# The inverse of each RWKV chunk multiplied into beta and the output weights ahead of the chain

## The chip, the core and the metric

The kernel runs on one core of a Trainium2 chip. The metric is the device time of one execution in microseconds (us). Engines are named as the profile names them: PE is the matrix engine (PEld its weight loads), DVE the vector engine, ACT the scalar engine, POOL and SP the other two; here SP issues nearly all DMAs.

## The reference, cut to what matters

The program is one layer of a bidirectional hybrid model: a modulated norm, an input projection, an RWKV-7 branch (16 heads of 64), a gated DeltaNet branch (8 heads of 128), a gated merge, and an MLP, over 256 latent and 256 context tokens. The change is inside the RWKV branch, whose recurrence for each head and direction is

```python
def step(s, inp):
    dec_t, k_t, v_t, kk_t, b_t = inp[:5]
    sa = jnp.einsum('bhvk,bhk->bhv', s, kk_t)
    s = (s * dec_t[:, :, None, :] - sa[..., None] * b_t[:, :, None, :]
         + v_t[..., None] * k_t[:, :, None, :])
    if with_out:
        return s, jnp.einsum('bhvk,bhk->bhv', s, inp[5])
    return s, None
```

It runs forwards and backwards over the context (state only) and then over the latent tokens (state and output). Each step reads the state that the step before left.

## The kernel before

The recurrence is done in chunks of 64 tokens: 8 chunks a direction, 4 of context and 4 of latent tokens. Two heads are worked on together as a *pair*, one in partitions 0 to 63 and one in 64 to 127; there are 8 pairs, and each has both directions. Within a chunk the dependence of the tokens on each other is a triangular system, so the work of a pair is in three generators:

- `prep2` makes, for all chunks, the decayed keys and betas (`ea`, `eb`), the triangular matrices (`dg` and `off`, their diagonal and off-diagonal 32x32 blocks), the transposed beta and key rows `bt`, and the output weights `mb`. Its products go to accumulators `pg`, of which there are two (`psg`, bufs=2).
- `inv2` inverts the 16 triangular 64x64 matrices of the pair: `tri_inv` does the 32x32 blocks in 31 steps on DVE, then two sets of small products (L818, L828) make the off-diagonal block, ACT copies the parts together into `ti`, and transposes of the values go into `vt`. Its accumulator `pr` is one (`psr`, bufs=1).
- `chain` goes through the 8 chunks in order, both directions side by side. A chunk has three products, each of which needs the one before: old state and values with `ea` or `eb` (L878), copied to `rs`; the inverse `ti` with `rs` (L896), copied into the tile `vu`; `bt` with `vu` (L912), from which DVE makes the next state. For latent chunks L917 and L919 add the output, the latter from `mb` and `vu`.

The function `weave` sets the order in which all of this is written. Its dense stream is the weight products of the projections: `mm3` (L239 to L241) does each weight tile in three products of a high and a low part, which `wgran` makes from the loaded weights, the high part on ACT (L226), the low part on DVE (L227). Into this stream `weave` puts steps of three lanes: the chains (first RWKV, then DeltaNet), the inverses, the preparations. A `yield` names how much dense work should pass until a lane's next step: CW = 1.5 between the products of a chain, times F_C = 1.5 for the chain's lane; Y[2] and Y[3] in `inv2`, times F_I = 0.7. Lanes wait for each other through sets: `chain` of a pair begins when the pair is in `done` (its `inv2` has ended), `inv2` of pair p when p - 2 is in `read` (that chain has ended), `prep2` likewise. The framework then orders the instructions of each engine by this order and by what is ready. When the RWKV chains are over, the DeltaNet heads follow with lanes of the same kind (`gprep`, `ginv`, `gchain`); the dense stream goes on with gates and up-projections `upa` (L1271 ends one). A DeltaNet head that ends before the gates do is written to memory and read again as `yr`, a later one goes straight to its place. Behind the weave come the branch merge, the output projection and the MLP, which the change doesn't touch.

## Time and profile before

| what | before |
| --- | --- |
| median of 3 runs | 2323.81 us (2322.46 to 2330.43) |
| the profiled execution's own time | 2331.12 us |
| its span | 2329.3 us |
| PE busy | 2218.4 us, 95% |
| DVE busy | 1581.7 us, 68% |
| ACT busy | 1353.9 us, 58% |
| DMA | 179 GB/s on average |

The span is the time from the first to the last recorded instruction of the profiled execution; the device time has a little around it. "Busy" is the union of an engine's instructions. A matrix product of two float32 operands is two PE instructions in the trace, one with the split weight products or a transpose is one.

### The profile page before, as it was taken

What the parts mean: (1) busy time and instruction counts of PE and PEld (TensorE: products, weight loads), DVE (VectorE), ACT (ScalarE), POOL (GpSimd) and SP (SyncE); (2) the same over time, 40 slices, a digit from 0 to 9 for tenths busy, and PEclk for the clock granted to TensorE, in tenths of its full rate; (3) what the DMA queues carried; (4) which work ended last, traced back from release to release, by engine and by line L of the source; (5) the groups of instructions that cost most, each with busy time, mean ns of one, the idle gap of its engine ahead of it and who ended that gap; (6) DMA issues with size and microseconds to landing.
All of it is one profiled execution on the core that took longest, in us unless ns stands there. A gap on an engine that the chain in (4) does not pass through costs nothing.

```text
span 2329.3 us, 45293 instructions
## 1 busy us (share of the span) xinstructions
PE 2218.4 (95%) x16886; PEld 1799.4 (77%) x16886; DVE 1581.7 (68%) x3590; ACT 1353.9 (58%) x3003; POOL 158.6 (7%) x343
## 2 busy tenths in 40 slices
PE   5989999999999999999999989999999999999997
PEld 1566676767677776778887889879998888999886
DVE  2366875858686867678577777776886555666555
ACT  3244758575758575766665676456555444555544
POOL 0000021111111121111000000000000000000000
PEclk9998999999999999999999999999999999999999
DMA  9953333423333333457676554875776666555654
GB/s 368 329 177 128 104 111 106 141 90 122 109 128 117 121 118 116 132 186 246 200 234 204 173 170 152 291 242 183 262 259 199 193 193 193 183 182 181 192 195 146
DMA packets 184372, 417.95 MB, mean 179 GB/s; under 512 B 15380, under 2 KB 37076, under 8 KB 183128
## 3 DMA queue, kind: packets, MB, share of 16 engines
q1 hardware_dynamic: 183576, 414.02, 54.3%
q8 instruction: 132, 2.16, 0.4%
q10 hardware_dynamic: 576, 1.05, 0.1%
q14 instruction: 88, 0.72, 0.1%
HBM read 399.63 MB, written 15.38 MB: 178 GB/s over the span
## 4 chain that ended last, share of the span: by engine, by line
PE 72%; ACT 8%; DVE 6%; DMA 4%; issue 2%; SPq 0%; DVEq 0%; ACTq 0%; POOL 0%; POOLq 0%
PE dacc L239 14%; PE dacc L240 13%; PE dacc L241 12%; PE dacc L1430 3%; PE pm L1428 3%; PE pm L1429 3%; PE pm L1430 3%; PE dacc L1428 3%; PE dacc L1429 3%; DMA raw<-in_mod_w_dram 2%; PE vacc L296 2%; DVE lo L227 2%; ACT hi L226 1%; PE cb L878 1%; PE pg L748 1%
## 5 line engine op out<-in xcount | busy, mean ns | idle before, releaser
L226 ACT CAST hi<-raw 128x512 fp32r<-128x512 f32 (+1 forms) x1032 | 628.1, 610 | 646.3 <-PE dacc L240 343.8
L227 DVE TENSOR_TENSOR lo<-raw,hi 128x512 fp32r<-128x512 f32 (+1 forms) x1032 | 695.2, 677 | 446.1 <-ACT hi L226 257.1
L239 PE MATMUL dacc<-hh,hi 128*128 128x256 f32 (+1 forms) x1648 | 562.8, 342 | 10.0 <-DVE sg L444 5.5
L241 PE MATMUL dacc<-hh,lo 128*128 128x256 f32 (+1 forms) x1648 | 532.4, 323 | 0.7 <-DVE lo L227 0.6
L240 PE MATMUL dacc<-hl,hi 128*128 128x256 f32 (+1 forms) x1648 | 532.1, 323 | 0.9 <-DVE hl L245 0.9
L239 PEld LDWEIGHTS dacc<-hh,hi 128*128 128x128 f32 x1648 | 315.2, 191 | 78.4 <-issue 39.6
L241 PEld LDWEIGHTS dacc<-hh,lo 128*128 128x128 f32 x1648 | 316.1, 192 | 25.7 <-issue 2.6
L240 PEld LDWEIGHTS dacc<-hl,hi 128*128 128x128 f32 x1648 | 316.3, 192 | 22.2 <-issue 3.4
L241 PE MATMUL dacc<-ah,lo 128*128 128x258 f32 x1024 | 291.7, 285 | 3.9 <-DVE lo L227 3.5
L239 PE MATMUL dacc<-ah,hi 128*128 128x258 f32 x1024 | 290.6, 284 | 1.1 <-ACT ah L244 1.1
L240 PE MATMUL dacc<-al,hi 128*128 128x258 f32 x1024 | 290.0, 283 | 0.0
L241 PEld LDWEIGHTS dacc<-ah,lo 128*128 128x128 f32 x1024 | 194.1, 190 | 6.6 <-DVE lo L227 5.6
L239 PEld LDWEIGHTS dacc<-ah,hi 128*128 128x128 f32 x1024 | 194.5, 190 | 2.4 <-ACT ah L244 1.3
L240 PEld LDWEIGHTS dacc<-al,hi 128*128 128x128 f32 x1024 | 194.2, 190 | 1.1 <-issue 1.0
L175 POOL TENSOR_SCALAR sp<-vu,pc 64x64 f32<-64x64 f32 x224 | 128.2, 572 | 433.3 <-DVE vu L175 381.0
L1430 PE MATMUL dacc<-lo,hh 128*128 128x512 f32 x320 | 125.7, 393 | 5.3 <-DVE lo L227 5.3
L1428 PE MATMUL dacc<-hi,hh 128*128 128x512 f32 x320 | 124.8, 390 | 1.6 <-ACT hi L226 1.6
L1428 PE MATMUL pm<-hi,hh 128*128 128x512 f32 x320 | 124.8, 390 | 0.0
L1430 PE MATMUL pm<-lo,hh 128*128 128x512 f32 x320 | 124.7, 390 | 0.0
L1429 PE MATMUL dacc<-hi,hl 128*128 128x512 f32 x320 | 124.7, 390 | 0.0
L1429 PE MATMUL pm<-hi,hl 128*128 128x512 f32 x320 | 124.6, 389 | 0.0
L485 DVE TENSOR_TENSOR ltmp<-X,Lt 128x126 f32<-128x126 f32 (+22 forms) x372 | 94.0, 253 | 7.3
(413 smaller groups left out, 3241.8 us busy)
## 6 DMA issues: line engine op xcount, KB each, us to landing
raw<-in_w_dram SPq DMA_DIRECT2D x256, 512.0 KB
raw<-in_mod_w_dram SPq DMA_DIRECT2D x96, 512.0 KB
graw<-in_mod_w_dram SPq DMA_DIRECT2D x96, 512.0 KB
raw<-in_w_gdn_dram SPq DMA_DIRECT2D x64, 512.0 KB
raw<-in_w_pg_dram SPq DMA_DIRECT2D x64, 512.0 KB
raw<-in_w_rkv_dram SPq DMA_DIRECT2D x40, 512.0 KB
raw<-in_out_w_dram SPq DMA_DIRECT2D x32, 512.0 KB
raw<-in_upa_dram SPq DMA_DIRECT2D x16, 512.0 KB
```

The costliest lines, as they stand in the source:

```text
L175: return getattr(self.eng, name)(*a, **k)
L226: S.copy(out=hi[:, :F], in_=x)
L227: V.tensor_tensor(out=lo[:, :F], in0=x, in1=hi[:, :F].bitcast(F32), op=ALU.subtract)
L239: P.matmul(out=o, lhsT=wh, rhs=ah, start=first, stop=False)
L240: P.matmul(out=o, lhsT=wh, rhs=al, start=False, stop=False)
L241: P.matmul(out=o, lhsT=wl, rhs=ah, start=False, stop=last)
L296: P.matmul(out=pm[32 * g:32 * g + 32, :], lhsT=sc_st[:, 2 * k:2 * k + 32], rhs=raws[g // 2][:, g % 2 * 512:g % 2 * 512 + 512], start=(q == ...
L485: V.tensor_tensor(out=tv, in0=X[:, 0:n, j:j + 1].to_broadcast([128, n, 31 - j]), in1=Lt[:, j:j + 1, j + 1:32].to_broadcast([128, n, 31 - j ...
L748: P.matmul(out=q[:, c], lhsT=bkh(h, 4 + c), rhs=eb[r, h, c], start=True, stop=True)
L1428: P.matmul(out=pss[i], lhsT=ah[:, tsl], rhs=wh, start=first, stop=False)
L1429: P.matmul(out=pss[i], lhsT=al[:, tsl], rhs=wh, start=False, stop=False)
L1430: P.matmul(out=pss[i], lhsT=ah[:, tsl], rhs=wl, start=False, stop=last)
```

## The change

`inv2` multiplies the transposed inverse into `bt` (32 products a pair, L841 of the changed kernel) and into `mb` (16 products, L850), with results copied back into the same tiles by ACT. The chain then copies the result of its first product straight into `vu`, and its second product (L922, before L912) reads the changed `bt`; the product with `ti` and the tile `rs` are gone. `inv2` now builds the transposed inverse, so the blocks of `ti` are filled in other places, and `xt` has a tile of its own.

```diff
--- before.py
+++ after.py
@@ -793,22 +793,25 @@
 
         def inv2(p, R):
 
+
             off = R["off"]
             ti = rp.tile([128, 16, 64], F32, tag="ti", name="ti", bufs=2)
-            xt = ti[:, :, 32:64]
+            xt = rp.tile([128, 16, 32], F32, tag="xt", name="xt")
             g = tri_inv(rp, R["dg"], xt)
             yield next(g)
             begun.add(p)
             X = yield from g
-            V.transpose(out=ti[:, 0:8, 0:32], in_=xt[:, 0:8, :])
-            S.copy(out=ti[:, 8:16, 0:32], in_=xt[:, 8:16, :])
             V.transpose(out=X[:, 0:8, :], in_=xt[:, 8:16, :])
+            V.transpose(out=X[:, 8:16, :], in_=xt[:, 0:8, :])
             halves = [[slice(64 * h + 32 * i, 64 * h + 32 * i + 32) for i in range(2)] for h in range(2)]
             for h in range(2):
-                a, b = halves[h]
-                S.copy(out=ti[b, :, 32:64], in_=ti[b, :, 0:32])
-                G.memset(ti[b, 0:8, 0:32], 0.0)
-                G.memset(ti[a, 8:16, 32:64], 0.0)
+                for i in range(2):
+                    b = halves[h][i]
+                    c = slice(32 * i, 32 * i + 32)
+                    S.copy(out=ti[b, 0:8, c], in_=xt[b, 0:8, :])
+                    S.copy(out=ti[b, 8:16, c], in_=X[b, 0:8, :])
+                G.memset(ti[halves[h][0], 0:8, 32:64], 0.0)
+                G.memset(ti[halves[h][1], 8:16, 0:32], 0.0)
             yield Y[2]
             q = pr()
             for u in range(8):
@@ -816,7 +819,7 @@
                     for d in range(2):
                         a, b = halves[h][::-1] if d else halves[h]
                         P.matmul(out=q[b, u * 32:(u + 1) * 32], lhsT=off[a, u, :], rhs=X[a, u, :] if d else xt[a, u, :], start=True, stop=True)
-            wt = X[:, 8:16, :]
+            wt = X[:, 0:8, :]
             S.copy(out=wt.rearrange("p u t -> p (u t)"), in_=q[:, :256])
             yield Y[3]
             q = pr()
@@ -824,13 +827,29 @@
                 for h in range(2):
                     for d in range(2):
                         a, b = halves[h][::-1] if d else halves[h]
-                        c = slice(32 - 32 * d, 64 - 32 * d)
-                        P.matmul(out=q[a, u * 32:(u + 1) * 32], lhsT=wt[b, u, :], rhs=ti[b, 8 * d + u, c], start=True, stop=True)
+                        P.matmul(out=q[b, u * 32:(u + 1) * 32], lhsT=xt[b, 8 + u, :] if d else X[b, 8 + u, :], rhs=wt[b, u, :], start=True, stop=True)
             for h in range(2):
                 for d in range(2):
                     a, b = halves[h][::-1] if d else halves[h]
-                    S.copy(out=ti[a, 8 * d:8 * d + 8, 32 - 32 * d:64 - 32 * d], in_=q[a, :256].rearrange("p (u t) -> p u t", t=32))
-            R["ti"] = ti
+                    S.copy(out=ti[b, 8 * d:8 * d + 8, 32 * d:32 * d + 32], in_=q[b, :256].rearrange("p (u t) -> p u t", t=32))
+            yield Y[3]
+            hr = [slice(0, 64), slice(64, 128)]
+            for d in range(2):
+                q = pg()
+                for n in range(8):
+                    for h in range(2):
+                        P.matmul(out=q[hr[h], n * 64:(n + 1) * 64], lhsT=ti[hr[h], d * 8 + n, :], rhs=R[d]["bt"][2 * h + n // 4][hr[h], n % 4, :], start=True, stop=True)
+                for h in range(2):
+                    for s2 in range(2):
+                        S.copy(out=R[d]["bt"][2 * h + s2][hr[h]].rearrange("p u t -> p (u t)"), in_=q[hr[h], s2 * 256:s2 * 256 + 256])
+                yield Y[3]
+            q = pg()
+            for d in range(2):
+                for n in range(4):
+                    for h in range(2):
+                        P.matmul(out=q[hr[h], d * 256 + n * 64:d * 256 + (n + 1) * 64], lhsT=ti[hr[h], d * 8 + 4 + n, :], rhs=R[d]["mb"][hr[h], n, :], start=True, stop=True)
+            for d in range(2):
+                S.copy(out=R[d]["mb"].rearrange("p u t -> p (u t)"), in_=q[:, d * 256:d * 256 + 256])
             yield Y[3]
             yield from until(lambda: p - 1 in loaded)
 
@@ -877,11 +896,9 @@
                     for h in range(2):
                         P.matmul(out=cbs[d][hr[h], 0:64], lhsT=r_["eb"][:, h, n - 4, 0, :] if c >= 4 else r_["ea"][:, h, n, :],
                                  rhs=vs_[d][:, n % 2, 0, h, :], start=True, stop=True)
-                rss = []
                 for d in range(2):
-                    rs = rp.tile([128, 64], F32, tag="rs", name="rs", bufs=2)
-                    S1.copy(out=rs, in_=cbs[d][:, 0:64])
-                    rss.append(rs)
+                    for h in range(2):
+                        S1.copy(out=vs_[d][hr[h], ns[d] % 2, 1, h, :], in_=cbs[d][hr[h], 0:64])
                 sps = []
                 for d in range(2):
                     sp_ = rp.tile([128, 64], F32, tag="sp", name="sp", bufs=3)
@@ -890,13 +907,6 @@
                         n = ns[d]
                         for h in range(2):
                             G1.tensor_scalar(out=sp_[hr[h]], in0=vs_[d][hr[h], n % 2, 0, h, :], scalar1=R[d]["pc"][hr[h], n:n + 1], scalar2=None, op0=ALU.mult)
-                yield CW
-                for d in range(2):
-                    for h in range(2):
-                        P.matmul(out=cbs[d][hr[h], 64:128], lhsT=R["ti"][hr[h], d * 8 + ns[d], :], rhs=rss[d][hr[h], :], start=True, stop=True)
-                for d in range(2):
-                    for h in range(2):
-                        S1.copy(out=vs_[d][hr[h], ns[d] % 2, 1, h, :], in_=cbs[d][hr[h], 64:128])
                 if c % 2 == 1 and c < 7:
                     yield CW / 2
                     nvs = [vload(d, sgm + 1) for d in range(2)]
```

How the order of PE's instructions differs is shown at two places of the fourth pair (p = 3). In these rows `dacc` is the weight products' accumulator, `hh` and `hl` the high and low parts of the activations, `hi` and `lo` those of the weights.

First, the chain of that pair; PE, before: a step with `ti`, and the next step.

```order
L896 MATMUL cb<-rs,ti 64x64 x4
L239 MATMUL dacc<-hh_128,hi 128x512
L240 MATMUL dacc<-hl_129,hi 128x512
L241 MATMUL dacc<-hh_128,lo 128x512
L751 MATMUL pg<-ea,bk 64x64 x16
L239 MATMUL dacc<-hh_130,hi 128x512
L240 MATMUL dacc<-hl_131,hi 128x512
L241 MATMUL dacc<-hh_130,lo 128x512
L239 MATMUL dacc<-hh_132,hi 128x512
L240 MATMUL dacc<-hl_133,hi 128x512
L241 MATMUL dacc<-hh_132,lo 128x512
L912 MATMUL cb<-vu,bt 64x64 x4
```

All four products of a step (two heads, two directions) stand together, with weight products and a group of the next preparation until the next step. PE, changed kernel, the chain of the same pair: L897 is the first product (before L878), L922 the second.

```order
L897 MATMUL cb<-vu,ea 64x64 x2
L240 MATMUL dacc<-hl_123,hi 128x512
L241 MATMUL dacc<-hh_122,lo 128x512
L897 MATMUL cb<-vu,ea 64x64 x2
L239 MATMUL dacc<-hh_124,hi 128x512
L240 MATMUL dacc<-hl_125,hi 128x512
L922 MATMUL cb<-vu,bt 64x64 x2
L241 MATMUL dacc<-hh_124,lo 128x512
L922 MATMUL cb<-vu,bt 64x64 x2
```

The two directions of a step now stand apart, with one or two weight products between. Second, the end of the pair's inverse; PE, before: L828 is the inverse's last product, L841 the first transposes of the values, L611 a product of a DeltaNet projection.

```order
L828 MATMUL pr<-ti,X 32x32 x32
L239 MATMUL dacc<-hh_116,hi 128x512
L611 MATMUL dacc<-gth,cs 128x256
L240 MATMUL dacc<-hl_117,hi 128x512
L241 MATMUL dacc<-hh_116,lo 128x512
L239 MATMUL dacc<-hh_118,hi 128x512
L240 MATMUL dacc<-hl_119,hi 128x512
L241 MATMUL dacc<-hh_118,lo 128x512
L239 MATMUL dacc<-hh_120,hi 128x512
L240 MATMUL dacc<-hl_121,hi 128x512
L241 MATMUL dacc<-hh_120,lo 128x512
L841 MATMUL pr<-cs,zv 64x128 x4
```

The transposes stand nine weight products behind the inverse. PE, changed kernel, the same place from the first new products on: L841 and L850 are new, L860 are the transposes, L676 is the next pair's decay product.

```order
L841 MATMUL pg<-bt,ti 64x64 x32
L860 MATMUL pr<-cs,zv 64x128 x4
L240 MATMUL dacc<-hl_133,hi 128x256
L241 MATMUL dacc<-hh_132,lo 128x256
L239 MATMUL dacc<-hh_102,hi 128x512
L240 MATMUL dacc<-hl_103,hi 128x512
L241 MATMUL dacc<-hh_102,lo 128x512
L239 MATMUL dacc<-hh_104,hi 128x512
L240 MATMUL dacc<-hl_105,hi 128x512
L850 MATMUL pg<-mb,ti 64x64 x16
L676 MATMUL pg<-tw,lw 128x512
L860 MATMUL pr<-cs,zv 64x128 x4
```

Four sets of products that use `pg` (L841 twice, L850, L676) and the transposes stand close together, with seven weight products among them.

## Rows read from the trace of the kernel before

**Rows 1.** The page: span, and each engine's busy time
```profile
span 2329.3 us, 45293 instructions
...
PE 2218.4 (95%) x16886; PEld 1799.4 (77%) x16886; DVE 1581.7 (68%) x3590; ACT 1353.9 (58%) x3003; POOL 158.6 (7%) x343
```

**Rows 2.** Busy time by stretch: the weave (columns in the first row)
```profile
core 0: us, PE busy (x) PEld busy (x) DVE busy (x) ACT busy (x) POOL busy (x), PEclk, DMA share, GB/s
...
290.00:1436.00 1146.00, 1100.48 (x9944) 858.58 (x9942) 832.08 (x2178) 760.39 (x1834) 147.87 (x310) 0.99 0.46 147
```

**Rows 3.** PE's timeline, one chunk of the fourth pair (start, length, instruction)
```profile
610.70 0.39 PE L240 MATMUL dacc<-hl,hi 128*128 128x512 f32 x1
610.93 0.39 PE L241 MATMUL dacc<-hh,lo 128*128 128x512 f32 x1
611.25 0.45 PE L896 MATMUL cb<-rs,ti 64*64 64x64 f32 x8
611.63 0.50 PE L239 MATMUL dacc<-hh,hi 128*128 128x512 f32 x1
611.97 0.39 PE L240 MATMUL dacc<-hl,hi 128*128 128x512 f32 x1
612.20 0.40 PE L241 MATMUL dacc<-hh,lo 128*128 128x512 f32 x1
612.52 0.69 PE L751 MATMUL pg<-ea,bk 64*64 64x64 f32 x32
613.15 0.50 PE L239 MATMUL dacc<-hh,hi 128*128 128x512 f32 x1
613.49 0.39 PE L240 MATMUL dacc<-hl,hi 128*128 128x512 f32 x1
```

**Rows 4.** Groups, 290 to 1436 us, PE: busy, mean ns | idle before
```profile
L896 PE MATMUL cb<-rs,ti 64*64 64x64 f32 x504 | 30.3, 232 | 0.3 <-ACT rs L175 0.3
L912 PE MATMUL cb<-vu,bt 128*64 128x64 f32 x440 | 27.0, 235 | 2.5 <-ACT vu L175 2.4
L878 PE MATMUL cb<-vu,ea 128*64 128x64 f32 x240 | 17.1, 236 | 0.9 <-ACT vu L175 0.8
L818 PE MATMUL pr<-ti,off 32*32 32x32 f32 x224 | 6.7, 195 | 2.5 <-DVE ti L488 2.5
L828 PE MATMUL pr<-ti,X 32*32 32x32 f32 x448 | 5.3, 194 | 0.7 <-ACT X L820 0.6
L841 PE MATMUL pr<-cs,zv 128*64 128x128 f32 x56 | 8.7, 277 | 2.7 <-ACT vt L843 2.1 <-ACT ti L832 0.5
...
L241 PE MATMUL dacc<-hh,lo 128*128 128x256 f32 (+1 forms) x1385 | 446.7, 323 | 0.3 <-DVE lo L227 0.2
```

**Rows 5.** PE's timeline and busy time, first pair's chain
```profile
295.07 0.50 PE L240 MATMUL dacc<-hl,hi 128*128 128x512 f32 x1
295.50 0.33 PE L896 MATMUL cb<-rs,ti 64*64 64x64 f32 x4
295.77 0.50 PE L241 MATMUL dacc<-hh,lo 128*128 128x512 f32 x1
...
282.00:310.00 28.00, 28.00 (x235) 18.59 (x232) 15.85 (x40) 18.27 (x66) 8.01 (x17) 1.00 0.29 95
```

**Rows 6.** Groups, 290 to 1436 us, ACT's copies and casts
```profile
L175 ACT COPY rs<-cb 128x64 f32<-128x64 f32 x126 | 21.5, 212 | 24.7 <-PE cb L878 16.4 <-DVE ltmp L485 2.9 <-issue 2.2
...
L226 ACT CAST hi<-raw 128x512 fp32r<-128x512 f32 x346 | 213.7, 618 | 208.9 <-PE dacc L240 172.6 <-issue 10.7 <-DVE X L487 6.3
...
L843 ACT COPY vt<-pr 64x256 f32<-64x256 f32 x28 | 10.2, 365 | 1.3 <-PE pr L841 0.8
```

**Rows 7.** PE's waits on the timeline, and the clock right after them
```profile
1435.66 0.38 PE L239 MATMUL dacc<-hh,hi 128*128 128x256 f32 x1 [1.15 <-ACT hh L244]
1436.50 0.54 PE L240 MATMUL dacc<-hl,hi 128*128 128x256 f32 x1 [0.45 <-DVE hl L245]
...
1436.60:1440.00 3.40, 3.40 (x16) 3.40 (x17) 3.13 (x20) 2.24 (x17) 0.00 (x0) 0.50 0.47 137
```

## The prediction, made before the changed kernel ran

> **What bounds the kernel now.** I read the page's busy table first: PE is busy for 95% of the span [rows 1]. The changed code runs only between about 290 and 1436 us, so I then cut the span there. In that stretch PE is busy for 1100.5 of 1146.0 us, VectorE for 832 and ScalarE for 760 [rows 2]. PE thus has 45.5 us of idle time, ScalarE some 386. The stretch is a weave: streams of weight products (L239 to L241) fill PE, and the small products of the recurrent chains are put between them. Third, the groups of instructions tell whether PE waits for the product that goes: its 504 instructions there had 0.3 us of idle time before them; the chain's two other products had 2.5 and 0.9 us [rows 4]. So a step of the chain is covered: while ScalarE makes its copies, PE streams weights. The chain is long but it isn't what ends the stretch; PE's own list of work is. The change must therefore be priced as PE work removed against PE work added, and then as waits.
>
> **Price of a small group.** The timeline of one chunk gives it. Two weight products that follow each other start 0.23 us apart (610.70, 610.93). With the removed group (4 products, 8 instructions) between, the starts 610.93 and 611.97 are 1.04 us apart in place of 0.46: it costs 0.58 us. The group of 32 instructions behind it costs 613.49 - 612.20 - 0.46 = 0.83 us [rows 3]. That one uses all four quarters of the array, so its 32 instructions are 8 steps; the removed one uses two quarters (one per head), so 8 instructions are 4 steps. From both: (0.83 - 0.58) / 4 = 0.0625 us a step, and 0.33 us for each change between wide and small products.
>
> **Removed.** 8 pairs x 8 chunks = 64 such groups at 0.58: **-37.1 us** on PE. With each go two copies `rs` of 212 ns on ScalarE [rows 6], 16 a pair.
>
> **Added.** A pair gets 32 products on `bt` (64 instructions in two quarters: 32 steps, 0.33 + 2.0 = 2.33 us) and 16 on `mb` (16 steps, 1.33 us): 8 x 3.66 = **+29.3 us**. In the order of the program some `bt` products stand alone, with weight products before the rest follows: I count 14 such pieces, 14 x 0.33 = **+4.6 us**. The products of the inverse itself are as many as before, and the memsets too.
>
> **Moved.** This decides the sign. The order (the first two pieces in the section on the change) shows that before, a chain step stands whole, with six to nine weight products until the next; now the two directions stand apart, with one or two weight products between. Counted over the program's order, 14 of 186 steps were split by weight products; now 47 of 117 are: 33 more. The reason is that a chain may start only when its own inverse is done, the inverse has become longer, and the chain before it now ends sooner; so the chain starts late and then runs close. The trace has such a stretch, the first pair's chain at 295 us: from 295.07 to 295.77 one weight product and one half step take 0.70 us, so a half step costs 0.47 and a split one 0.94, which is 0.36 more than a whole [rows 5]. 33 x 0.36 = 11.9 us if each weight product between had nothing else to wait for, 0 if the halves fill holes in which no weight was ready. I take **+9 us**, nearer to the row, in which PE doesn't idle.
>
> A page of the Trainium skill bears on this (TensorEngine Tiling (Array Packing), Key Properties): a change of tiling mode drains the engine, whatever the number of products behind it. The 0.33 us agrees. Counted by the diff alone, that rule is in favour: 64 changes go and 24 come; counted by the program's order it isn't, since the 14 pieces and 33 splits eat the difference.
>
> **Waits.** PE's idle time before the three products of the inverse stage (L818, L828, L841) is 2.5 + 0.7 + 2.7 us over 7 pairs, 0.28 us a product and pair [rows 4]. The new products add three places where PE can wait: `bt` for the last copies into `ti`; `mb` for a free accumulator of `pg`, of which there are two, both taken by `bt`; and the next pair's decay product (L676) for the other one. The first takes the place of a wait that the transposes of `vt` have now, so two are new: 16 x 0.28 = **+4.5 us**. The bounds are 0 and, if all eight copies of 365 ns must end first (the nearest copies of that shape [rows 6]), about 2 us a pair, 16 us. Behind `mb` and L676 on PE queue the next transposes and the chain's first step, so nothing passes such a wait. The chain's waits of 0.3 + 2.5 + 0.9 us lose a third: **-1.2 us**. At the end of the stretch PE waited 1.15 + 0.45 us for the last DeltaNet head [rows 7]; the chains now end sooner, while gates and up-projections go on, so this goes, and with it the half clock behind it, 3.4 us at 0.5: **-3.3 us**. In its place all 8 heads go through memory (16 reads of `yr`, 13 before); three reads of 128 KB lie beside weight products.
>
> **At nothing:** ScalarE gets 18 copies a pair of about 0.36 us (6.6 us) for 16 of 0.212 and three larger ones: under 3.2 us a pair net, some 26 us in all against 386 idle. If that cover fails, the cast to `hi` is late and the weight products wait; now 1385 of them had 0.3 us of such waits together [rows 4]. The queues of SP and POOL keep the chain's order.
>
> **Sum:** -37.1 + 29.3 + 4.6 + 9 + 4.5 - 1.2 - 3.3 = **+5.8 us**. The profiled execution took 2331.12 us (span 2329.3), 7.3 us over the median of the three runs, 2323.81. The sum is a difference, so I put it on the median: **2330 us**.
>
> **Rivals.**
> *Slower: the accumulators.* Place: the order's third and fourth pieces. Before, nine weight products stand between the inverse's last product and the transposes; now `bt`, transposes, seven weight products, `mb` and L676 follow each other. Eight copies of 0.365 are 2.9 us behind the `bt` products, and the transposes, weight products and `mb` cover about 1 to 2 us of it, less when a cast of 618 ns comes between [rows 6]; PE then stands 2 us a pair, 16 us in place of 4.5. Where PE had stood for 1.15 and 0.45 us, its clock was at half (1.2 of 2.4 GHz) for the next 3.4 us [rows 7]; in 4 of 8 pairs that is 4 x 1.7 = 6.8 us more. 2330 + 11.5 + 6.8 = **2348 us**. It decides from 1 us of wait a pair. Against it: the three waits seen now are short. The same page of the Trainium skill (PSUM Bottleneck) says that tiling speeds up the products and not the copies out of PSUM, so that these may become the bound; the 2.9 us of copies for 2.3 us of product agree, no run yet shows the wait.
>
> *Faster: the splits are free.* The halves were put where no weight product was ready, and PE would have idled there; for it speaks that in the first pair's close stretch, 282 to 310 us, PE is busy for 28.00 of 28.00 us at full clock [rows 5]. Against: there PE is full, so the changes cost. Without splits and without new waits: 5.8 - 9 - 4.5 = -7.7: **2316 us**.
>
> *The shorter chain does nothing.* It never was the bound, and PE's exchange comes out even, since removed and added steps are of one size: **2324 us**.
>
> **How the numbers follow.** About 0.3%, 7 us, is what a measurement of this kernel can tell from no change; 2330 lies just inside. My forecast holds with 0.46: 0.27 within 7 us, 0.17 slower, 0.02 faster. The accumulators get 0.20, all slower. Free splits get 0.22: 0.14 faster, 0.08 within. The even exchange gets 0.12: 0.06 within, 0.03 to each side. Together 0.19 faster, 0.41 within, 0.40 slower. The forecast's own range is 2321 to 2339 (splits 0 to 11.9, waits 0 to 10). The range goes from 2313, beyond the free splits, to 2349, the accumulators' case.
>
> **What would show it.** In the new profile the chain's first product is followed at once by the four copies into `vu` and has no idle time over 1 us in the group; `bt` and `mb` products take about 2 and 1 us a pair; PE's count of instructions rises by 256. The stretch still has PE busy for 95% or more, and the last DeltaNet chain ends ahead of its last up-projections. I'm wrong if PE's idle time in the stretch falls or rises by more than 8 us, if the wait is at weight products (casts late), or if the time after 1436 us changes.

## The result, and the profile after

The changed kernel takes 2387.01 us (2379.77 to 2397.70, 4 runs) against 2323.14 for the kernel before: a ratio of 1.0262 (1.0228 to 1.0295). 2330 was forecast, with a range to 2349. The profiled execution took 2382.70 us. First the page of the changed kernel:

```profile
span 2380.9 us, 45815 instructions
...
PE 2251.5 (95%) x17142; PEld 1819.1 (76%) x17142; DVE 1581.7 (66%) x3590; ACT 1375.4 (58%) x2997; POOL 170.0 (7%) x343
```

PE has the 256 instructions more that were counted, and 33 us more of busy time [rows 1]. Where does the time sit? The first instruction of the branch merge, which no edit touches, starts at 1438.8 us before and at 1495.1 after; what follows it takes 890.5 and 885.8 us. All of the loss lies ahead of the merge. The two profiled executions lie 51.6 us apart, the medians 63.9, so what follows splits up most of the loss and not all of it. The stretch to split up is the one from 190 us to the merge. The columns are those of [rows 2]; before:

```profile
190.00:1438.80 1248.80, 1196.97 (x10610) 925.87 (x10610) 907.12 (x2368) 824.97 (x1981) 153.63 (x328) 0.98 0.44 143
```

and after, with its last 76 us by themselves:

```profile
190.00:1495.10 1305.10, 1229.23 (x10880) 947.06 (x10880) 909.09 (x2363) 847.32 (x1973) 165.02 (x328) 0.98 0.43 139
...
1419.00:1495.10 76.10, 63.89 (x480) 61.85 (x479) 45.39 (x94) 38.96 (x87) 0.00 (x0) 0.94 0.58 178
```

Length less busy time is PE's idle time: 51.8 us before, 75.9 after, +24.1. The clock record has 39.8 us at half clock in this stretch before and 61.0 after; half of each is lost, +10.6. What is left, PE's work as it would be at full clock, is 1197.0 - 19.9 = 1177.1 before and 1229.2 - 30.5 = 1198.7 after, +21.6. The three add up to the 56.3. By this reckoning more than half of the loss isn't work of PE.

The groups of the changed kernel from 290 to 1495 us (most of the first pair's products stand ahead of 290 us and aren't counted here):

```profile
L296 PE MATMUL vacc<-graw,sc_st 128*32 128x512 f32 x344 | 73.4, 623 | 8.1 <-DMA graw<-in_mod_w_dram 8.1
...
L922 PE MATMUL cb<-vu,bt 128*64 128x64 f32 x416 | 28.2, 238 | 1.0 <-ACT vu L175 0.8
...
L897 PE MATMUL cb<-vu,ea 128*64 128x64 f32 x224 | 19.8, 242 | 1.8 <-ACT vu L175 0.9 <-DVE vu L175 0.8
...
L841 PE MATMUL pg<-bt,ti 64*64 64x64 f32 x448 | 18.7, 222 | 1.8 <-ACT ti L834 1.8
...
L676 PE MATMUL pg<-tw,lw 96*128 96x512 f32 x26 | 14.5, 638 | 2.3 <-ACT bt L782 2.2 <-ACT bt L844 0.2
L678 PE MATMUL pg<-xa,lw 128*128 128x512 f32 x26 | 13.8, 612 | 1.6 <-ACT bt L782 1.6
...
L850 PE MATMUL pg<-mb,ti 64*64 64x64 f32 x224 | 8.0, 221 | 0.4 <-ACT bt L844 0.3
...
L821 PE MATMUL pr<-xt,off 32*32 32x32 f32 x224 | 7.1, 201 | 5.9 <-DVE xt L488 5.9
```

The chain's products wait little, as before [rows 4]. New waits stand where `pg` is handed on (L850, and L676 and L678, the first products of the next preparation: 4.3 us together), at L841 for the copies into `ti` (1.8), and at the inverse (L821 took the place of L818). The largest stands where no edit was made: L296, the products of the modulation weights, waits 8.1 us for their reads (`graw`), and its busy time is 14 us longer than before with as many instructions. Before:

```profile
L296 PE MATMUL vacc<-graw,sc_st 128*32 128x512 f32 x344 | 59.3, 605 | 0.6 <-DMA graw<-in_mod_w_dram 0.6
```

Of the twelve stretches at half clock up to the merge three (at 345, 813 and 885 us) begin at such a wait. Why these reads come late wasn't tested.

The other engines show the chain more clearly. DVE's waits in this stretch for products of the RWKV chain (L912 and L919 before, L922 and L929 after; columns: in all, times, longest), before:

```profile
DVE vu L175 <- PE cb L912: 8.2, 11, 2.9
DVE vu L175 <- PE cb L919: 6.7, 13, 1.5
```

and after:

```profile
DVE vu L175 <- PE cb L922: 34.4, 20, 6.4
DVE vu L175 <- PE cb L929: 17.0, 16, 3.6
```

The chain of a pair now runs close: from its first to its last state product (L878, L897) a pair takes 79 to 92 us before (the first pair 54) and 32 to 60 after. One such place, on PE's timeline of the changed kernel:

```profile
608.09 1.04 PE L296 MATMUL vacc<-graw,sc_st 128*32 128x512 f32 x2
...
611.40 0.33 PE L929 MATMUL cb<-mb,vu 64*64 64x64 f32 x4
612.51 0.54 PE L897 MATMUL cb<-vu,eb 128*64 128x64 f32 x8 [0.78 <-DVE vu L175]
613.37 0.34 PE L922 MATMUL cb<-vu,bt 128*64 128x64 f32 x4 [0.32 <-ACT vu L175]
...
614.72 1.03 PE L611 MATMUL dacc<-gth,cs 128*128 128x256 f32 x2
...
617.76 1.92 PE L296 MATMUL vacc<-graw,sc_st 128*32 128x512 f32 x2
...
620.41 0.79 PE L239 MATMUL dacc<-hh,hi 128*128 128x512 f32 x1
```

DVE in the same microseconds:

```profile
611.35 0.28 DVE L175 SCALAR_TENSOR_TENSOR vu<-cb,pc,sp 64x64 f32<-64x64 f32 x1 [1.20 <-PE cb L929]
...
617.61 0.60 DVE L175 SCALAR_TENSOR_TENSOR vu<-cb,pc,sp 64x64 f32<-64x64 f32 x2 [1.88 <-PE cb L929]
```

and the busy times before and after 615 us:

```profile
608.20:615.00 6.80, 5.70 (x63) 3.13 (x63) 4.94 (x13) 4.07 (x13) 3.03 (x5) 1.00 0.47 156
615.00:621.80 6.80, 6.80 (x37) 3.67 (x37) 3.47 (x10) 4.78 (x11) 3.80 (x11) 0.50 0.04 14
```

From 608 to 620 us none of the products of L239 to L241 stands on PE, only shorter groups, with 1.1 us of waits between them up to 615.0; there the granted clock falls to 0.50, the lower of its two levels, and the 1.04 us of a piece of L296 become 1.92. The Trainium skill (TensorE: Matmul & The Clock Gate, What's actually happening) says that the clock is granted by how busy the array has been; the trace agrees as far as it goes: PE had 0.9 to 3.5 us of waits in the 7 us ahead of each of the twelve stretches at half clock, but a wait of 1.8 us at 322 us has none behind it.

The end of the stretch shows the opposite. The last product of a DeltaNet head (L1250 before, L1260 after) starts at 1430.2 us before, 8.6 us ahead of the merge, and at 1418.7 after, 76 us ahead of it. PE's waits in these 76 us:

```profile
PE dacc L239 <- DVE gu L1281: 6.1, 5, 2.1
PE dacc L239 <- ACT hh L244: 5.7, 3, 2.3
```

The two longest of them on the timeline:

```profile
1430.42 0.51 PE L239 MATMUL dacc<-hh,hi 128*128 128x256 f32 x2 [1.62 <-ACT hh L244]
...
1434.63 0.80 PE L239 MATMUL dacc<-hh,hi 128*128 128x256 f32 x2 [2.29 <-ACT hh L244]
```

ScalarE's cast to `hh` (L244), for which PE waits there, waits itself for a head's result to be read back from memory (`yr`). ScalarE's waits for these reads in the 76 us:

```profile
ACT hh L244 <- DMA yr<-ysp: 6.6, 5, 3.5
```

The 76 us have 12.2 us of idle time and 10.2 us at half clock (5.1 lost). Before, the tail behind the last head had 1.6 and 3.4 [rows 7], 14 us less; an equally long last 76 us had 7.8 us idle and 2.2 at half clock, so by that count the tail costs some 8 us.

### The profile page after: what moved, and what is told of

Its sections match the earlier page's. It is cut to its first block, busy times and chain, and to the rows that moved or that the text cites. A ratio compares the mean times of both kernels' runs of the same rounds, so it can differ in the third digit from the quotient of the medians.

```text
span 2380.9 us, 45815 instructions
## 1 busy us (share of the span) xinstructions
PE 2251.5 (95%) x17142; PEld 1819.1 (76%) x17142; DVE 1581.7 (66%) x3590; ACT 1375.4 (58%) x2997; POOL 170.0 (7%) x343
## 4 chain that ended last, share of the span: by engine, by line
PE 69%; DVE 8%; ACT 8%; DMA 4%; issue 2%; DVEq 0%; ACTq 0%; SPq 0%
PE dacc L239 13%; PE dacc L240 12%; PE dacc L241 12%; PE dacc L1440 3%; PE pm L1439 3%; PE pm L1438 3%; PE pm L1440 3%; PE dacc L1438 3%; PE dacc L1439 3%; PE vacc L296 2%; DVE lo L227 2%; DMA raw<-in_mod_w_dram 2%; ACT hi L226 1%; DVE X L487 1%; PE cb L897 1%
## 5 line engine op out<-in xcount | busy, mean ns | idle before, releaser
L239 PE MATMUL dacc<-hh,hi 128*128 128x256 f32 (+1 forms) x1648 | 551.6, 335 | 25.0 <-DVE gu L1281 6.1
L240 PE MATMUL dacc<-hl,hi 128*128 128x256 f32 (+1 forms) x1648 | 539.5, 327 | 0.0
L241 PE MATMUL dacc<-hh,lo 128*128 128x256 f32 (+1 forms) x1648 | 537.0, 326 | 0.9 <-DVE lo L227 0.9
L239 PEld LDWEIGHTS dacc<-hh,hi 128*128 128x128 f32 x1648 | 317.6, 193 | 91.5 <-issue 42.9
L241 PEld LDWEIGHTS dacc<-hh,lo 128*128 128x128 f32 x1648 | 318.0, 193 | 25.7 <-issue 3.5
L241 PE MATMUL dacc<-ah,lo 128*128 128x258 f32 x1024 | 291.5, 285 | 3.7 <-DVE lo L227 3.7
L239 PE MATMUL dacc<-ah,hi 128*128 128x258 f32 x1024 | 290.5, 284 | 0.0
L241 PEld LDWEIGHTS dacc<-ah,lo 128*128 128x128 f32 x1024 | 194.2, 190 | 6.6 <-DVE lo L227 5.9
L239 PEld LDWEIGHTS dacc<-ah,hi 128*128 128x128 f32 x1024 | 194.5, 190 | 1.0 <-issue 1.0
L175 POOL TENSOR_SCALAR sp<-vu,pc 64x64 f32<-64x64 f32 x224 | 140.2, 626 | 543.9 <-DVE vu L175 491.6
L175 DVE SCALAR_TENSOR_TENSOR vu<-cb,pc,sp 64x64 f32<-64x64 f32 x224 | 60.8, 282 | 73.8 <-PE cb L922 37.4
```

Of the source, the lines that this page charges most:

```text
L175: return getattr(self.eng, name)(*a, **k)
L239: P.matmul(out=o, lhsT=wh, rhs=ah, start=first, stop=False)
L240: P.matmul(out=o, lhsT=wh, rhs=al, start=False, stop=False)
L241: P.matmul(out=o, lhsT=wl, rhs=ah, start=False, stop=last)
```

## The experiments

In the table *idle* is the length of the stretch from 190 us to the merge less PE's busy time, *half* the time at half clock in it, *work* busy time less half of that: all from one profiled execution each. That execution lies within 8 us of its kernel's median, but for before_plus_products (10.5 us below) and one_accumulator_175 (14.5 above). Where PE is idle at half clock, *work* comes out too low: by 12 us in before_pace_2, 11 in one_accumulator_3, and at most 4 elsewhere. Ratios are to the kernel before, timed beside each, and where the text gives the price of a kernel in us without two medians, it is its ratio on 2326 us.

| kernel | median us | ratio (95%) | work | idle | half |
| --- | --- | --- | --- | --- | --- |
| before | 2321.7 to 2329.8 | 1 | 1177 | 52 | 40 |
| changed | 2387.0 | 1.0262 (1.0228 to 1.0295) | 1199 | 76 | 61 |
| pace225 | 2353.5 | 1.0111 (1.0082 to 1.0141) | 1167 | 70 | 68 |
| no_products | 2330.5 | 1.0015 (0.9995 to 1.0035) | 1150 | 67 | 74 |
| no_products_225 | 2313.0 | 0.9938 (0.9909 to 0.9967) | 1145 | 68 | 31 |
| before_plus_products | 2379.2 | 1.0233 (1.0193 to 1.0273) | 1211 | 62 | 34 |
| products_alone | 2366.2 | 1.0177 (1.0145 to 1.0208) | 1205 | 60 | 34 |
| copies_alone | 2318.4 | 0.9974 (0.9959 to 0.9990) | 1173 | 51 | 31 |
| four_quarters_225 | 2371.8 | 1.0199 (1.0173 to 1.0225) | 1157 | 84 | 109 |
| one_accumulator_225 | 2342.7 | 1.0067 (1.0045 to 1.0089) | 1167 | 70 | 51 |
| before_pace_1 | 2363.4 | 1.0161 (1.0118 to 1.0204) | 1197 | 58 | 58 |
| before_pace_2 | 2387.5 | 1.0261 (1.0220 to 1.0301) | 1167 | 85 | 121 |
| one_accumulator | 2353.7 | 1.0125 (1.0079 to 1.0171) | 1186 | 54 | 68 |
| one_accumulator_3 | 2378.6 | 1.0220 (1.0182 to 1.0258) | 1163 | 92 | 77 |
| hold_pg | 2360.8 | 1.0159 (1.0134 to 1.0185) | 1171 | 85 | 64 |
| hold_pr | 2347.0 | 1.0099 (1.0072 to 1.0126) | 1167 | 64 | 68 |
| before_plus_products_one_accumulator | 2352.6 | 1.0119 (1.0081 to 1.0157) | 1206 | 50 | 34 |
| one_accumulator_175 | 2338.4 | 1.0083 (1.0052 to 1.0114) | 1188 | 56 | 58 |
| later_off_products | 2360.8 | 1.0130 (1.0088 to 1.0173) | 1176 | 72 | 72 |
| later_off_products_225 | 2343.3 | 1.0072 (1.0046 to 1.0099) | 1175 | 66 | 38 |

### Pace and products, each with and without the other

```diff
-CW, F_C, ... = 1.5, 1.5, ...          # pace225 (changed kernel)
+CW, F_C, ... = 2.25, 1.5, ...
-            (the bt and mb products and their ten copies)   # no_products, at CW 1.5 and 2.25
```

*pace225.* 

> The changed kernel with one number altered: CW = 2.25 in place of 1.5, so that a chunk's two chain steps take as much of the weave as three did (2 x 2.25 = 3 x 1.5). Theory 1 (pace): the loss of 64 us comes from the chains running ahead of their inverses and then close together, with PE waits and half-clock stretches behind them, and from a tail without chains; the work itself exchanges at about +9 us. It expects 2325 to 2342 us. Theory 2 (work): the products on bt and mb and their copies cost the 64 us wherever the chain's steps stand; it expects 2380 to 2395. Theory 3 (accumulators): PE stands before mb and L676 because pg has two buffers; it expects 2370 to 2390, since the inverse stage is unchanged.

*no_products.* 

> The changed kernel without the products of the inverse on bt and mb and without their copies (the inverse's effect is left out of the recurrence); the chain has two products a chunk at the changed kernel's pace. Theory 1 (pace) expects it still slower than before, since the chains still bunch: 2387 less about 24 us of product work, 2350 to 2370. Theory 2 (work) and theory 3 (accumulators) expect it faster than before, by the 37 us of the product that went from the chain: 2280 to 2305.

*no_products_225.* 

> As the run without the products, but with CW = 2.25. Theory 1 (pace) expects 2290 to 2312 (before less 15 to 37 us of PE work). Theories 2 and 3 expect the same time as without the products at CW = 1.5, within 10 us.

The pace gave back 33.5 us with the products and 17.5 without. At 2353.5 and 2330.5 the first two kernels came out between what a loss by pace alone and one by work or accumulators alone would have given, so none of the three explains the loss by itself. The two kernels without products leave the inverse out of the recurrence, and so do hold_pg and hold_pr below. Without the products, and at the better pace, the kernel is only 14 us faster than before, though PE's work fell by 32: idle time rose from 52 to 68 us.

```profile
190.00:1419.20 1229.20, 1160.72 (x10104) 904.03 (x10103) 902.17 (x2368) 816.85 (x1892) 157.80 (x328) 0.99 0.44 145
```

```diff
 # before_plus_products: the kernel before, at the end of inv2
+            bx = rp.tile([128, 512], F32, tag="bx", name="bx")
+            (the 48 products as in the changed kernel; the ten copies go to bx)
```

*before_plus_products.* 

> The kernel before, unchanged chain, with the same 32 + 16 products a pair on bt and mb after the inverse, their results copied to a scratch tile that nothing reads. It measures the work alone, with three products in the chain. Theory 1 (pace): 24 to 36 us more than before, 2345 to 2360. Theory 2 (work) expects over 90 us more (the 64 of the change and the 37 that the chain's product gave back): 2400 to 2430. Theory 3 (accumulators): as theory 2, since the accumulators are used in the same way.

*products_alone* (without the copies). 

> The kernel before with the 32 + 16 products a pair added, without the copies of their results (nothing reads them). With products and copies it was 52 us slower. Theory PE-work: most of it is here, 8 x 3.66 us and some single pieces: 28 to 40 us over before, 2352 to 2366. Theory copies (ScalarE's queue is what hurts): under 15 us, 2326 to 2340.

*copies_alone* (ten copies of `bt` and `mb` to `bx`, no product). 

> The kernel before with the ten copies a pair added on ScalarE at the same place (from the unchanged bt and mb to a scratch tile), without the products. Theory PE-work: 0 to 10 us over before, 2325 to 2335. Theory copies: 30 to 45 us over before.

Beside the old chain the products add 28 to 33 us of PE work, about as worked out, but cost 40 us without copies and 52 with them; the 52 are more than the 24 to 36 of the pace theory and far from the 90 of the others. The copies alone cost nothing: 8 us less, though each takes 0.40 us of ScalarE where those of the changed kernel take 0.37. A new order of the program is the likely reason, not a shown one; it says how much of a small difference not to believe.

### The accumulators

```diff
 # one_accumulator (CW 1.5), _175, _225, _3; hold_pr; before_plus_products_one_accumulator
-                q = pg()
+                q = pr()
 # four_quarters_225, at CW 2.25: both directions' products side by side
+            qd = [pg() for _ in range(2)]
+            ... P.matmul(out=qd[d][hr[h ^ d], n * 64:(n + 1) * 64], lhsT=ti[hr[h], d * 8 + n, :], ...)
```

*one_accumulator_225.* 

> The changed kernel with CW = 2.25 and the new products in the accumulator pr of the inverse (one buffer) and not in pg, so the next pair's preparation never meets them. Theory accumulators: the waits at mb and at the next pair's decay product go, 10 to 16 us less than 2353: 2337 to 2343. Theory PE-work: the same within 5 us, 2348 to 2358; slower still if the single buffer makes the products wait for their own copies, up to 2375.

*four_quarters_225.* 

> The changed kernel with CW = 2.25 and the new products in all four quarters of the array: direction 1 of each head goes to the other half of the accumulator, the two directions alternate, so 64 instructions are 16 steps and not 32 (bt), 32 are 8 and not 16 (mb). Same products, copies and accumulators. Theory PE-work (what is left at CW = 2.25 is the new products' time on PE): 24 steps fewer a pair, 8 x 24 x 0.0625 = 12 us less than the 2353 us at CW = 2.25: 2337 to 2345. Theory accumulators (PE stands for the two buffers of pg and their copies): unchanged, 2349 to 2358.

*one_accumulator.* 

> The changed kernel at its own pace (CW 1.5), with the new products in the accumulator pr of the inverse, in place of pg. Accumulators as the first cause: most of the waits that the change brought go, 2387 - 25 or more, so 2362 or less. Pace as the first cause and accumulators as a second, independent one: the same 10.8 us as at CW 2.25, 2372-2381. Accumulators only matter when the chain is spread: no change, 2383-2392.

At the changed kernel's own pace `pr` in place of `pg` takes off 33 us, as much as the pace did in `pg`; at 2.25 it takes off 11. The time is in the branch *accumulators as the first cause* (2362 or less). But both edits together take off 44 us, and each alone 33: some 22 us of the loss go with either, and the runs can't say which of the two comes first. In one_accumulator's profile the waits for `pg` at the next preparation are gone, and those for the modulation weights:

```profile
L296 PE MATMUL vacc<-graw,sc_st 128*32 128x512 f32 x344 | 63.6, 613 | 0.1
...
L676 PE MATMUL pg<-tw,lw 96*128 96x512 f32 x24 | 13.1, 627 | 0.0
L678 PE MATMUL pg<-xa,lw 128*128 128x512 f32 x24 | 12.6, 604 | 0.0
```

The stretch up to the merge there:

```profile
190.00:1464.60 1274.60, 1220.10 (x10875) 949.64 (x10874) 902.98 (x2360) 847.85 (x1969) 149.84 (x328) 0.97 0.43 141
```

Idle time fell by 21.4 us, work by 13. The pieces of L676, L678, L841 and L850 are only 3.5 us of the idle time, the wait for `graw` is 8.1, and L296 has 9.8 us less of busy time; so most of the gain stands at places that don't use `pg`, and how they hang on it isn't shown. DVE's waits for the chain stayed (49.4 us, 51.4 in the changed kernel): they don't set this price. The four quarters hold both accumulators of `pg` twice a pair. PE's work fell by 10 us against pace225, as fewer steps should make it, and the time rose by 18, all of it idle time (+14) and half clock (+41); both expectations were too low. The Trainium skill (TensorEngine Tiling (Array Packing), PSUM Bottleneck) says that copies out of PSUM may become the bound once tiling has sped up the products; here PE waits 2.0 us at L678 and 1.1 at L851 for such copies, so the waits are there, but the run doesn't show that they are the bound.

```diff
 # hold_pg, hold_pr: changed kernel at CW 1.5, one product of four or eight stays, all ten copies go to bx
-                for n in range(8):
+                for n in range(1):
```

*hold_pg.* 

> The changed kernel at its own pace with the accumulators' use kept and most of the products' work taken out: 8 of the 48 new products of a pair remain (one of each head, direction and half), all ten copies stay, at their size of 256 elements, but go to a tile that nobody reads, so beta and the output weights stay without the inverse. In pg as in the changed kernel; hold_pr is the same in pr, and the two differ by the accumulator alone. Without products it was 2330.5; the 8 products and their changes of mode are some 1.2 us a pair, 10 us. Accumulators theory: the wait for pg is bound to the copies and not to the products, so hold_pg is 20 to 33 us over hold_pr, 2355-2373. Rival (pg costs only through the 48 products' own time, or through the order that they bring): within 8 us of hold_pr.

*hold_pr.* 

> As hold_pg (8 of 48 new products, ten copies to a tile that nobody reads), with pr in place of pg. Both theories: 2330.5 + 10, so 2333-2348. If the waits are those of the inverse's own accumulator, pr is held for longer here and this is the slower of the two.

The stretch up to the merge in hold_pg:

```profile
190.00:1478.00 1288.00, 1202.77 (x10232) 930.40 (x10231) 906.31 (x2359) 845.10 (x1968) 156.09 (x328) 0.98 0.43 140
```

and in hold_pr:

```profile
190.00:1455.30 1265.30, 1201.52 (x10223) 930.72 (x10219) 898.95 (x2355) 846.60 (x1968) 148.27 (x328) 0.97 0.44 142
```

Nearly the same work (1171 and 1167), and 21 us more of idle time with `pg`: 13.8 us in the medians, less than the 20 to 33 expected, more than the rival's 8. The two profiled executions lie 25 us apart, so the 21 us overstate it. This speaks for an accumulator that costs by being held, with the products' own time on top; it is not far beyond the 8 us that an order can bring.

*before_plus_products_one_accumulator.* 

> The kernel before plus the new products and their ten copies to a tile that nobody reads (that cost 52.5 us in pg, where 33.9 were worked out), in pr in place of pg. Accumulators theory, at any pace: 10 to 33 us less than in pg, 2346-2369, about the 33.9 of the products' own work over before. Rival (pg hurts only beside a chain that is run close): 2372-2386, no change.

It came down from +52 to +31 us: the 29 us of PE work that the products add, and little more. So `pg` is dearer than `pr` in all four pairs of kernels that differ in nothing else, by 33, 11, 14 and 22 us, and in each pair L296 is busy for 7 to 11 us longer with `pg`. Taking the chain's product away from this kernel, and letting the chain read the results, gives one_accumulator, and that has the same time (1.0119 and 1.0125). Work fell by 20 us, idle time rose by 4.6, and half clock rose by 34, which costs 17.

### The pace by itself

*before_pace_1* (the kernel before, CW 1.0). 

> The kernel before, unchanged but for the pace: CW 1.0 in place of 1.5, so that its three steps take as much of the program's time per chunk (3 x 1.0) as the two steps of the changed kernel do (2 x 1.5). No product is removed or added. Pace theory (a chain run at its own latency holds its in-order engines, and PE waits and falls to half clock behind it): a pair's chain shrinks from 80 to 90 us to about 45, and the time rises by the 17 to 33 us that pace cost in the changed kernel, to 2343-2360. Rival (the loss is the products' own and what they make late; pace only matters together with them): within 0.3% of before, 2320-2333.

PE's timeline of one chunk:

```profile
599.78 0.34 PE L878 MATMUL cb<-vu,ea 128*64 128x64 f32 x4
600.05 0.51 PE L240 MATMUL dacc<-hl,hi 128*128 128x512 f32 x1
600.48 0.34 PE L878 MATMUL cb<-vu,ea 128*64 128x64 f32 x4
600.75 0.33 PE L896 MATMUL cb<-rs,ti 64*64 64x64 f32 x4
601.01 0.50 PE L241 MATMUL dacc<-hh,lo 128*128 128x512 f32 x1
601.44 0.33 PE L896 MATMUL cb<-rs,ti 64*64 64x64 f32 x4
```

DVE's waits for this chain:

```profile
DVE vu L175 <- PE cb L912: 34.6, 33, 3.7
DVE vu L175 <- PE cb L919: 9.6, 14, 1.7
```

The old chain, run at the new chain's length of 39 to 57 us a pair, loses 37 us: its halves are split (in the trace a product of L239 to L241 stands inside 86 of its 184 steps, 15 before), DVE waits nearly as in the changed kernel, and the last chain ends 83 us ahead of the merge. Work rose by 20.0 us for 71 more split steps, 0.28 us each if nothing else added to it.

*before_pace_2* (CW 2.0). 

> The kernel before with CW 2.0. Pace theory: at 1.5 its chain has 80 to 90 us a pair already and is not bunched, so nothing is left to gain: 2316-2331. Rival (a slower pace gains by itself, in any kernel, so that the gain of the changed kernel at 2.25 tells nothing about the change): 2313 or less, as the changed kernel without products gained 17.5 us.

This missed both: 61 us slower. Here the chains end last. From 1396 us on, the weights are used up, and 73 of the 121 us at half clock lie there:

```profile
1395.80:1502.80 107.00, 71.89 (x576) 59.49 (x576) 47.56 (x156) 49.81 (x132) 1.03 (x2) 0.66 0.05 16
```

*one_accumulator_175.* 

> The changed kernel with the products in pr and CW 1.75, between 1.5 (2353.7) and 2.25 (2342.7). If the time follows the pace smoothly: 2346-2354. If each pace is a new order with gains and losses of its own (before went up by 36 and 60 us on either side of 1.5): anywhere from 2335 to 2385, and no statement on pace can be built on one point. Below 2323 would beat before.

*one_accumulator_3.* 

> The changed kernel with the products in pr and CW 3.0. Pace theory: the gain is used up once the chain has some 75 us of a pair's 110, so no more than a few us to the 2342.7 at CW 2.25: 2336-2350. If waits of the chain were still the larger part at 2.25, it goes on falling: 2325-2335. If a chain that is too slow holds up the next pair's inverse and the end of the stretch: over 2350.

At 1.75 the time is below both ends that were expected from a smooth curve (2346 to 2354), by 8 us, as much as a new order can bring; 2.25 and 1.75 can't be told apart. At 3.0 the last branch came out: a chain that is too slow holds up the end, and idle time is 92 us. Of the paces tried each kernel has a best one, 1.5 before and 1.75 or 2.25 in the changed kernel with `pr`, and the time is higher on both sides of it: the change moved that value. Where the last chain ends doesn't mark it: 8.6 us ahead of the merge before, 9.5 in one_accumulator_225, but 74 in one_accumulator_175, which is as fast.

### The inverse's wait

```diff
-Y = (2, 2.5, 2, 2, 0, 1)
+Y = (2, 2.5, 5, 2, 0, 1)        # changed kernel with pr, CW 1.5 and 2.25
```

*later_off_products.* 

> The changed kernel with the products in pr, at CW 1.5, and one number of the planner more: the inverse's yield ahead of its first off-diagonal products (L821) is 5 in place of 2, so that more weight products stand ahead of them. In the profile of one_accumulator PE waits there for VectorE's transpose xt in every pair (9.9 us, 8 times), and four of these waits have a stretch at half clock behind them. If this wait, with its half clock, is part of what eats the gain of the shorter chain: 9.9 + some 4 to 8 us less, 2336-2344 from 2353.7. Rival (the wait only moves to the next product of the inverse or the chain): no change, 2348-2360.

*later_off_products_225.* 

> The same at CW 2.25 (one_accumulator_225: 2342.7, 7.4 us of these waits in 7 pairs, three with half clock behind). If the wait counts: 2329-2336; at the most level with before. Rival: 2338-2348, so that the 16 us over before stay.

PE's waits at L821 in one_accumulator:

```profile
PE pr L821 <- DVE xt L488: 9.4, 7, 1.9
```

and in later_off_products:

```profile
PE pr L821 <- DVE xt L488: 10.5, 7, 2.9
```

At 2.25 it is 6.9 us without the edit and 7.0 with it. The number didn't reach the wait, and neither kernel got faster, so both runs say nothing about it. What it is worth stays open.

## Why the prediction was wrong

By steps, as fractions of the 61 us (the ratio on 2326 us): the products' accumulator 32 (1.0262 to 1.0125), the pace 13 (to 1.0067 at CW 2.25), and 16 left that neither takes away. In the other order the pace takes 35 and the accumulator 10.

**The step that failed first is *Waits*.** Its three terms, +4.5, -1.2 and -3.3, come to nothing; measured were +24.1 us of idle time and 10.6 lost to the clock, 34.7 of the 56.3 us. PE's work was to rise by 5.8 and rose by 21.6. The wait for an accumulator of `pg` was named at its place, and valued at two rows of 0.28 us a pair, 4.5 us, since L818, L828 and L841 waited no longer than that. It is worth 11 us (CW 2.25) to 33 us (CW 1.5). The rival *accumulators* had the place and the queue behind it (2348), and its 16 us of waits and 6.8 of half clock lie within that range. But it had them at L850 and L676, where the direct wait was short, 4.3 us with L678, and not at what gets later elsewhere, such as the 8.1 us of waits for the modulation weights; the rows of PE's waits for the three products of the inverse couldn't give the price of delay. How the delay gets from `pg` to those other places stays open. So does what an order does by itself: each of these edits also gives the program a new order, and copies_alone, 8 us off, is the only run near to that question.

**The close chain** was seen under *Moved* and priced at its splits alone. Spreading it again (CW 2.25) takes off 33.5 us, as much as the other accumulator: the waits and the half clock of a close chain had no term.

**The second is the end of the stretch, -3.3 us.** That the chains would end ahead of the up-projections was right. That PE's waits go with them was wrong: of the 12.2 us of idle time there 6.1 are for VectorE's product behind an up-projection (`gu`) and 5.7 for ScalarE's casts, which had waited for the reads of `yr`. These reads, 16 for 13, were put beside weight products at no cost. 8 to 14 us were lost there, by what one compares with, where 3.3 were to be gained. The tail isn't what decides, though: one_accumulator_175 has it too (74 us) and is among the fastest. The forecast kept the pace fixed while the chain lost a third of its steps; before_pace_1 has the same tail and the same close chain, without any edit of the products.

**The third is the removal's worth as time.** PE's work was priced well part by part: the removal takes 32 us off (no_products_225; -37.1 expected), the products add 28 to 33 (29.3 + 4.6 expected), and at CW 2.25 the whole exchange makes PE's work 10 us smaller. But what was removed seems to have been lying in time that PE, without it, partly waits: idle time at CW 2.25 is 70 us against 52, with or without the new products (70 and 68), and half clock 51 against 40. 10 us less work, 18 us more idle time and 6 us of half clock give the 14 that this stretch lost. The reading "PE's list of work ends the stretch" took 45 us of idle time for a constant. It isn't one: it runs from 50 to 92 us in the table. That it depends on how much short work lies between the weights is argued, not shown.

**Splits, +9 us.** Right in count: in the trace 50 of the changed kernel's 120 steps are split and 15 of 184 before, 35 more for the 33 counted. The price is less sure: 0.28 us by before_pace_1 where 0.36 was worked out, so 10 us; but hold_pr has 34 more split steps than hold_pg and no more work. That splits are free is unlikely, and it wasn't the cause that mattered. **The even exchange** is out: the time moved by 61 us. Of the 21.6 us that PE's work rose in the changed kernel, the priced terms (-37.1 + 29.3 + 4.6 + 10) give 7; the other 15 are about as much as L296 alone is busy longer (59.3 to 73.4), a product that no term had. **At nothing**, for ScalarE's copies, held where they stand alone (copies_alone); beside the products they go with 12 us (40 to 52). The transfers that SP issues, also at nothing, weren't free: the reads of the modulation weights and of `yr` came late, and PE waited 8.1 us for the first and 5.7 behind the second.

No version that computes the whole beats the kernel before beyond doubt. The best of the changed kernels, with `pr` and a pace of 2.25, is at 1.0067; copies_alone, at 0.9974, is the old kernel with work that nobody uses.

## What to carry to other kernels

When a step is taken out of a chain that is woven into a stream, tune the pace again before judging: of the paces tried the old chain had its best at 1.5, and 0.5 to either side cost 37 and 61 us here. Don't price an accumulator by the wait that the trace shows at its next user; try the new products in another one first. Look through all of PE's waits, also at products that the change doesn't touch. And when PE is 95% busy, removed work may come back as waits and half clock, so forecast work, idle time and clock apart.

## What the runs showed of the hardware

Waits of PE can cost more than themselves: each of the twelve stretches at half clock in the changed kernel, 61 us in all, stands behind 0.9 to 3.5 us of waits. Half clock comes to 109 us in four_quarters_225 and to 121 in before_pace_2. A chain step split in two by weight products goes with 0.28 us more of PE work in before_pace_1 (71 steps, 20.0 us). The 344 instructions of L296 keep PE busy for 59.3, 63.6 or 73.4 us, by the kernel that they stand in.
